# Layer 1's feed-forward input product as seven half products instead of eight

## The chip, the cores and the metric

The kernel runs on one core of one Trainium2 chip. The metric is device time in microseconds (us) of one execution. The engines are named as the profile names them: PE (TensorE, matmuls), DVE (VectorE), ACT (ScalarE), POOL (GpSimd) and SP, whose queue issues the loads of weights.

## The reference, cut to what matters

The model has two layers over 1024 latent tokens (and 256 context tokens, which layer 1 only reads). Layer 1 ends so, with 1024 channels and 2816 hidden columns:

```python
x = _layer_norm(DN_ALPHA * x + g_m * y_lat, ln_g[layer, 0], ln_b[layer, 0])   # y_lat: HGRN2's output projection
f_lat = _conv_ffn(x * (1.0 + sc_f) + sh_f, ffn_w_in[layer], ffn_conv_w[layer],
                  ffn_conv_b[layer], ffn_w_out[layer])
x = _layer_norm(DN_ALPHA * x + g_f * f_lat, ln_g[layer, 1], ln_b[layer, 1])
```

`_conv_ffn` splits u @ w_in (1024 to 2 x 2816) into a and g, runs a centred depthwise convolution of width 3 over the tokens of a, and returns (silu(conv(a)) * g) @ w_out (2816 to 1024). Everything is float32.

## The kernel before, in words

Tokens lie along the free dimension and channels on partitions. A float32 product is made of three matmuls: each operand is held as a high and a low part (`split` L108 to L113: high by ACT L110, low by a subtraction in L113, on POOL for weights and on DVE for `hl`), and `mm3` L100 to L104 adds high times high (L102), high times low (L103) and low times high (L104) in one PSUM bank. The modulated activations u are two tiles, `uh` and `ul`, of [128, 8 channel tiles, 1280 tokens].

Weights come by `wload` (L312 to L325): one transfer of 512 KB by SP into one of two staging places `ws`, then ACT L110 and POOL L113 write the two parts into one of three places `w`.

`ffn` (L1070 to L1180) walks over 22 hidden tiles t of 128 columns. Of each tile, `values` makes the a product for two blocks of 512 tokens (`into`: 8 channel tiles, three matmuls each, into `pa`), and ACT L1118 copies it out; `product` makes the g product the same way into `pg`. `hidden` then runs on DVE and ACT: the convolution in three DVE steps (L1133, L1134, L1135), silu on ACT (L1136), the product with `pg` on DVE (L1137), and the split into `hh` (ACT L110) and `hl` (DVE L113). `out` takes two hidden tiles at a time into `po` (eight pieces of six matmuls for each block), and `gate` (DVE L1065) adds each piece to `acc`.

In front of it stands `Mix1.rest` (the output projection of HGRN2, `pmix`) with `norm` L1013 to L1060 behind each block of columns: sums over channels on PE (`pmean` L1025, `pvar` L1039, `prstd` L591), subtraction, scaling and `rstd` on DVE (L1030, L1045, L578 to L585), the modulated value on ACT, POOL (L1052) and DVE (L1053). The block of tokens 512 to 1024 comes last and in two parts of 256, so the first two hidden tiles run ahead on the tokens that are done. Behind the last hidden tile stand the second `norm` and `store` (L1525 on), which transposes on PE (`pout` L1537) and copies out on ACT (L1538).

The order of the instructions on each engine is not the order of the program text: a scheduler that simulates a timeline sets it, and the pools (places for tiles, banks of PSUM) add the waits.

Of the kernel before, what the change touches and what calls it, by code (L numbers as in the profile page):

```python
# [46 lines left out]
def constants():  # L47
    """Tables that depend on shapes alone."""
# [31 lines left out]
class Pool:  # L80
    """A pool of tiles whose life is not a block of the program text."""
# [12 lines left out]
def raw(t, off, dims):  # L94
    """An access pattern over all partitions of a tile."""
    pstride = t.ap[0][0]
    return bass.AP(tensor=t.tensor, offset=t.offset + off, ap=[[pstride, t.shape[0]]] + dims)


def mm3(nc, ps, w, x, start, stop):  # L100
    """ps (+)= w^T x of float32 operands that come as (hi, lo)."""
# [5 lines left out]
def split(nc, hi, lo, src, ehi="a", elo="p"):  # L107
    """hi = src rounded to twelve bits, lo = the rest: both exact."""  # L108
# [7 lines left out]
def merge(*gens):  # L116
    """Emit the steps of several generators evenly: (number of steps, generator)."""
# [8 lines left out]
def behind(k, inst):  # L126
    """What follows is issued after this instruction, where it is of the same engine."""
# [7 lines left out]
# which banks of PSUM a product goes to: the streams of a phase take theirs apart  # L135
# [9 lines left out]
# ---------------------------------------------------------------- setup  # L145

def setup(k, A):
# [31 lines left out]
    # columns of the small vectors  # L179
# [38 lines left out]
def lower_bounds(k, A, S):  # L218
    """One minus the lower bound of layer 1's forget gates, [128, dir, head]; the masks of its levels."""
# [25 lines left out]
def ada_steps(k, A, pool, layer, c0, nw, wtag=None):  # L245
    """Columns c0 .. c0+4*nw of the modulation of both streams."""
# [60 lines left out]
def wload(k, pool, src, n, tag="w", bufs=3, sbufs=2, elo="p", size=1024, spool=None, stag=None):  # L307
    """A piece of weights [128, kt, m] as (hi, lo)."""
# [13 lines left out]
def exp_small(k, P, o, x, n):  # L322
    """exp to float32's accuracy: 2^k times a polynomial, for a few columns."""
# [22 lines left out]
# ---------------------------------------------------------------- S5 set-up  # L346

def s5_setup(k, A, P, late):
    """late: four places of T columns, in use until this is done."""
# [49 lines left out]
    # powers 0..8 of lambda: [128, part, power, (d p)]  # L399
# [12 lines left out]
    def cmul(o0, n_, a0, b0):  # L412
        """powers o0.. = powers a0.. times power b0"""
# [14 lines left out]
    # input factors (fr, fi)  # L428
# [14 lines left out]
    # the powers for one, two and four chunks of eight tokens  # L443
# [3 lines left out]
    # C, transposed to [(q n), pair, channel]  # L447
# [16 lines left out]
    # B of the discrete system: [(q n), (d pair), channel]  # L464
# [16 lines left out]
    # block diagonal B: [(q n), (q c)] of each pair  # L481
# [11 lines left out]
    for h in range(4):  # L493
        psz[h] = [bank(k, "psz", "C") for d in range(2)]
        for d in range(2):
# [25 lines left out]
            # what a carried state adds to position j: power j+1 forward, 8-j backward  # L521
# [4 lines left out]
            # taps: forward lags 0..7 = index 0..7, backward lags -7..0 = index 1..8  # L526
# [8 lines left out]
            # input matrices: position j enters with power 7-j forward, j backward  # L535
# [26 lines left out]
    # one token of a chunk sees the taps from its own position on  # L562
# [25 lines left out]
def bcast_cols(k, ps, cols, n):  # L588
    """ps[p, 128 i + t] = cols[t, i] for all p."""
# [5 lines left out]
def rot_copy(k, s, kt, m, x0, r0):  # L595
    """staged weights [128, kt, m]: columns r0.. = the rotated partner of columns x0.."""
# [9 lines left out]
def in_proj(k, A, wp, places):  # L606
# [10 lines left out]
    def groups(ms):  # L617
        """The state-space layer's input, eight tokens to a row."""
# [17 lines left out]
    # kr and its rotated partner  # L636
# [54 lines left out]
# ---------------------------------------------------------------- layer 0: attention and S5  # L691

def attention(k, A):
# [18 lines left out]
    # V of all heads  # L712
# [22 lines left out]
    def qk(h):  # L735
# [30 lines left out]
        for s, e in BLK:  # L766
# [14 lines left out]
            # the maximum of every query's scores, negated, in row 96  # L781
# [27 lines left out]
    def attend(h):  # L809
        b = h % 2  # L810
        q, kk_, v = QT[b], KT[b], Vt[b]
        for s, e in BLK:
# [17 lines left out]
            # the sums of the exponentials stay beside the products and divide them later  # L830
# [10 lines left out]
    def inverse(h, s, e):  # L841
        """The reciprocals of two heads' sums."""
# [27 lines left out]
class S5Half:  # L870
    """The state-space layer, sixteen groups at a time, in steps that other work can run between."""
# [802 lines left out]
```

## Time and profile before

| what | value |
|---|---|
| median of three executions | 3871.06 us |
| lowest, highest | 3857.05 us, 3872.54 us |
| the profiled execution: span on the core | 3858.9 us (the page gives no other time of it) |
| PE busy | 3615.2 us, 94% of the span |
| DVE, POOL, ACT busy | 2055.3, 1133.2, 1090.3 us |
| layer 1's feed-forward part, from the end of the last `pmix` to the end | 3044.4 to 3858.9 us |

The span runs from the first to the last instruction that the profiler recorded. The profile names instructions by line, engine and operation, with the tiles that they write and read (out<-in, buffer numbers left out). Matmuls overlap: a matmul of 512 columns is shown as 0.39 us long, while the next one starts 0.23 us later, so the rate is read from starts, or from the count in a window that is 100% busy.

### The profile page before, as it was taken

How to read it: one execution, taken by the hardware profiler on the slowest of the kernel's cores; microseconds unless marked ns; L12 is line 12 of the kernel's file. 1: busy time of each engine (PE TensorE's matmuls, PEld its weight loads, DVE VectorE, ACT ScalarE, POOL GpSimd, SP SyncE). 2: the span in 40 equal slices, each digit the busy share in tenths (PEclk: the TensorE clock that was granted, in tenths of full speed). 3: DMA queues.
4: the chain of work that ended last, by engine and by line, in shares of the span. 5: the costliest groups of instructions: out<-in, count | busy, mean ns of one | idle time of the engine just before them, and what ended most of it. 6: DMA issues, size and time to landing. Idle time of an engine off the chain costs nothing.

```text
span 3858.9 us, 47479 instructions
## 1 busy us (share of the span) xinstructions
PE 3615.2 (94%) x19057; PEld 2924.6 (76%) x19057; DVE 2055.3 (53%) x3297; ACT 1090.3 (28%) x1798; POOL 1133.2 (29%) x1089
## 2 busy tenths in 40 slices
PE   6987999997399999999999899999998999999997
PEld 4764566565278888888888798989887978888886
DVE  7726745773246444444445756464645654444445
ACT  2323435444224111111111522222222421212113
POOL 3617613851144111111112611111112621222222
PEclk8998999998699999999999999999999999999997
DMA  7362335312211111111110201101013111111111
GB/s 239 120 172 80 112 95 134 112 32 94 88 50 44 39 33 39 33 34 49 39 39 28 77 28 33 36 31 39 31 46 95 50 52 42 55 44 50 44 44 44
DMA packets 297079, 245.69 MB, mean 64 GB/s; under 512 B 42488, under 2 KB 257354, under 8 KB 295834
## 3 DMA queue, kind: packets, MB, share of 16 engines
q1 hardware_dynamic: 291930, 229.97, 20.0%
q10 hardware_dynamic: 4928, 12.69, 0.9%
q8 instruction: 149, 2.44, 0.3%
q14 instruction: 72, 0.59, 0.0%
HBM read 206.39 MB, written 38.32 MB: 63 GB/s over the span
## 4 chain that ended last, share of the span: by engine, by line
PE 80%; DVE 6%; DMA 4%; POOL 2%; issue 1%; SPq 1%; ACT 1%; ACTq 0%; DVEq 0%; POOLq 0%
PE pa L104 5%; PE pa L102 5%; PE pa L103 5%; PE po L102 5%; PE pg L102 5%; PE pg L104 5%; PE po L103 5%; PE po L104 5%; PE pg L103 5%; PE ph L103 3%; PE ph L104 3%; PE ph L102 3%; PE pA L1425 3%; PE pY L964 2%; DMA rt<-rsd 2%
## 5 line engine op out<-in xcount | busy, mean ns | idle before, releaser
L113 POOL TENSOR_TENSOR w<-ws,w 128x1024 fp32r<-128x1024 f32 (+1 forms) x205 | 500.2, 2444 | 1570.6 <-ACT w L110 1460.5
L1065 DVE SCALAR_TENSOR_TENSOR acc<-po,mod,acc 128x512 f32<-128x512 f32 (+1 forms) x456 | 309.3, 679 | 560.3 <-PE po L104 560.0
L102 PE MATMUL po<-hh,w 128*128 128x512 f32 (+1 forms) x912 | 342.9, 377 | 9.9 <-DVE acc L1065 8.2
L103 PE MATMUL po<-hl,w 128*128 128x512 f32 (+1 forms) x912 | 336.3, 369 | 5.8 <-DVE hl L113 5.8
L104 PE MATMUL po<-hh,w 128*128 128x512 f32 (+1 forms) x912 | 335.6, 368 | 0.0
L110 ACT ACTIVATE w<-ws 128x1024 fp32r<-128x1024 f32 (+1 forms) x207 | 217.0, 1049 | 409.2 <-PE pg L104 165.7
L102 PE MATMUL pa<-uh,w 128*128 128x512 f32 (+1 forms) x896 | 331.7, 370 | 0.9 <-ACT w L110 0.8
L103 PE MATMUL pa<-ul,w 128*128 128x512 f32 (+1 forms) x896 | 330.1, 369 | 0.1
L104 PE MATMUL pa<-uh,w 128*128 128x512 f32 (+1 forms) x896 | 326.4, 370 | 0.8 <-POOL w L113 0.8
L102 PE MATMUL pg<-uh,w 128*128 128x512 f32 (+1 forms) x872 | 324.1, 372 | 1.9 <-ACT w L110 1.9
L103 PE MATMUL pg<-ul,w 128*128 128x512 f32 (+1 forms) x872 | 322.7, 370 | 0.0
L104 PE MATMUL pg<-uh,w 128*128 128x512 f32 (+1 forms) x872 | 321.5, 372 | 0.6 <-POOL w L113 0.6
L102 PE MATMUL ph<-uh,w 128*128 128x512 f32 (+1 forms) x624 | 239.5, 384 | 1.3 <-ACT uh L1051 1.3
L103 PE MATMUL ph<-ul,w 128*128 128x512 f32 (+1 forms) x624 | 235.6, 378 | 0.8 <-DVE ul L1053 0.8
L104 PE MATMUL ph<-uh,w 128*128 128x512 f32 (+1 forms) x624 | 235.0, 377 | 0.0
L102 PEld LDWEIGHTS po<-hh,w 128*128 128x128 f32 x912 | 174.1, 191 | 45.2 <-DVE acc L1065 11.1
L103 PEld LDWEIGHTS po<-hl,w 128*128 128x128 f32 x912 | 174.4, 191 | 37.9 <-DVE hl L113 6.9
L104 PEld LDWEIGHTS po<-hh,w 128*128 128x128 f32 x912 | 174.2, 191 | 30.3
L102 PEld LDWEIGHTS pa<-uh,w 128*128 128x128 f32 x896 | 168.7, 188 | 32.7 <-ACT w L110 1.0
L104 PEld LDWEIGHTS pa<-uh,w 128*128 128x128 f32 x896 | 168.6, 188 | 32.2 <-POOL w L113 1.3
L103 PEld LDWEIGHTS pa<-ul,w 128*128 128x128 f32 x896 | 168.5, 188 | 32.2 <-DVE ul L1053 0.4
L102 PEld LDWEIGHTS pg<-uh,w 128*128 128x128 f32 x872 | 164.1, 188 | 35.6 <-ACT w L110 2.3
(399 smaller groups left out, 7894.3 us busy)
## 6 DMA issues: line engine op xcount, KB each, us to landing
ws<-in_ffn_w_in_dram SPq DMA_DIRECT2D x88, 512.0 KB
adaw<-in_ada_w_dram SPq DMA_DIRECT2D x80, 512.0 KB
ws<-in_ffn_w_out_dram SPq DMA_DIRECT2D x44, 512.0 KB
ws<-in_hg_w_in_dram SPq DMA_DIRECT2D x40, 512.0 KB
w<-in_ada_w_dram SPq DMA_DIRECT2D x8, 1024.0 KB
ws<-in_ev_w_out_dram SPq DMA_DIRECT2D x10, 512.0 KB
ws<-in_hg_w_out_dram SPq DMA_DIRECT2D x10, 512.0 KB
ws<-in_ev_w_in_dram SPq DMA_DIRECT2D x9, 512.0 KB
```

The source lines that it names most:

```text
L102: nc.tensor.matmul(ps, lhsT=w[0], rhs=x[0], start=start, stop=False)
L103: nc.tensor.matmul(ps, lhsT=w[0], rhs=x[1], start=False, stop=False)
L104: return nc.tensor.matmul(ps, lhsT=w[1], rhs=x[0], start=False, stop=stop)
L110: nc.scalar.activation(hi, src, AF.Copy)
L113: (nc.gpsimd if elo == "p" else nc.vector).tensor_tensor(lo, src, hi.bitcast(F), op=OP.subtract)
L964: nc.tensor.matmul(ps[:, :160], lhsT=O[64 * q:64 * q + 64, d, i], rhs=H[64 * q:64 * q + 64, d:d + 160, d, i, p], start=d == 0 and i == 0, ...
L1065: k.nc.vector.scalar_tensor_tensor(a, ps[:, :e - s], modcol(k, layer, seg, 1 if s >= SEQ else 0, ct), a, op0=OP.mult, op1=OP.add)
L1425: nc.tensor.matmul(ps[:, i * 128:i * 128 + 128], lhsT=km[:, c:c + 128], rhs=raw(Q, c, [[2 * hs, 64 // hs], [SEQ + hs, 2], [1, hs]]), start ...
```

## The change

Layer 1 gets a function of its own, `ffn7`. Two hidden tiles of a (or of g) form a group of 256 columns, so the product of a group is a matrix of 2 x 2 blocks: channel halves against the two hidden tiles (weights A11, A21, A12, A22) and channel halves against the two blocks of tokens (activations B11, B21 and the two of the second block). By Strassen's scheme (in Winograd's form) the four results come from seven half products of 4 x 3 matmuls, 84 in all, where the kernel before ran 96. The operands of the products are A11, A12, A22, S1 = A21 + A22, S2 = S1 - A11, S3 = A11 - A21, S4 = A12 - S2 on the weights' side, and B11, B21, T1, T2, T3, T4 and B22 on the other.

- The S are formed for every group on DVE in the staging places, then split: highs on ACT, lows on DVE for S and on POOL for A11, A12 and A22. A group takes two transfers of 512 KB and four places of the ring `w`, which still has three; the pair's two `w_out` pieces take two more. There are three staging places in place of two.
- The T are formed once, from both blocks, behind the norm: 16 subtractions and 12 lows on DVE, 16 highs on ACT, 4 lows and 4 of B22's on POOL.
- Sums of products are made where possible by accumulating a second product into the same bank; what is left are three to four additions a group on DVE (L1365, L1371, L1393 for a, L1417 for g) and a copy on ACT. The convolution's first step moves from DVE (L1133) to ACT (L1402).
- u is one tile `X` in parts by channel half and block (class `Cols`), so that B's parts are tiles of their own; the norm's temporary tiles share places with `hh` and `hl`. HGRN2's output projection keeps three of its weights instead of four, and loads one a second time. The stretch of memory that is kept for descriptors is set to 1024 bytes.
- `out` has two banks of its own, products turn through the six others. All of the last pair's `out` stands behind the last product.

```diff
+class Seven:
+    def ops(self):
+        k, nc, V, G = self.k, self.k.nc, self.k.nc.vector, self.k.nc.gpsimd
+        for j in range(4):
+            (a, b), t = (r[j] for r in self.raw), self.temps(j)
+            T1, T2, T3, T4 = t
+            V.tensor_tensor(T1, b[:, 0], a[:, 0], op=OP.subtract)
+            V.tensor_tensor(T2, b[:, 1], T1, op=OP.subtract)
+            V.tensor_tensor(T3, b[:, 1], b[:, 0], op=OP.subtract)
+            V.tensor_tensor(T4, a[:, 1], T2, op=OP.subtract)
...
+            for i, (o, x) in enumerate(((self.T2, T2), (self.T3, T3), (self.T1, T1), (self.T4, T4))):
+                split(nc, o[j][:, 0], o[j][:, 1], x, elo="p" if i == 3 else "v")
...
+    def weights(p, i):
...
+        t1, t2, t3 = tile(), tile(), tile()
+        put("A11", t1[0], A11, "p")
+        put("A12", t1[1], A12, "p")
+        put("A22", t3[1], A22, "p")
+        V.tensor_tensor(A22, A21, A22, op=OP.add)
+        V.tensor_tensor(A21, A11, A21, op=OP.subtract)
+        V.tensor_tensor(A11, A22, A11, op=OP.subtract)
+        put("S2", t2[0], A11, "v")
+        put("S3", t2[1], A21, "v")
+        put("S1", t3[0], A22, "v")
+        V.tensor_tensor(A12, A12, A11, op=OP.subtract)
+        t4 = tile()
+        put("S4", t4[0], A12, "v")
...
+        def run(self, begun=False):
...
+            product(b, w["S2"], B.T2, True)
+            V.tensor_tensor(u, u, b, op=OP.add)
+            if not begun:
+                self.second()
+            c = inbank()[:]
+            product(c, w["S3"], B.T3, True)
+            u3 = temp()
+            V.tensor_tensor(u3, u, c, op=OP.add)
+            d = inbank()[:]
+            product(d, w["S1"], B.T1, True)
+            self.to(1, 1, u3, d)
+            product(c, w["A22"], B.T4, False)
+            self.to(1, 0, u, c)
+            product(d, w["S4"], B.B22, False)
+            self.to(0, 1, u, d)
...
+    ga = values(0)
+    ga.first()
+    gg = hidden(0)
+    for p in range(NP):
+        if p == 0:
+            ga.second()
+            ga.run(True)
+        else:
+            ga = values(p)
+            ga.run()
+        if p:
+            ws = [wout(p - 1, i) for i in range(2)]
+            for b in range(2):
+                out(p - 1, ws, b)
+        for j in range(2):
+            conv(p, j)
+        if p:
+            gg = hidden(p)
+        gg.run()
+    ws = [wout(NP - 1, i) for i in range(2)]
+    for b, part in ((0, (0, 512)), (1, (512, 768)), (1, (768, 1024))):
+        out(NP - 1, ws, b, part)
+        done(*part, b == 1)
```

Three places show how the order moves.

PE behind the last `pmix`, around the inverse deviation (`prstd`) of the last 256 tokens. Before, `pa` is the a product of a hidden tile on 256 tokens that are normed already:

```order
L102 MATMUL pa<-uh,w 128x256
L103 MATMUL pa<-ul,w 128x256
L591 MATMUL prstd<-ident,lnr 128x128 x2
L104 MATMUL pa<-uh,w 128x256
L102 MATMUL pa<-uh,w 128x256
```

After, `pi` is any of the seven products, `X_23583` holds T2, the other `X` here T3, and `c_23591` T1:

```order
L1336 MATMUL pi<-X,w 128x512
L1059 MATMUL pvar<-ones,hh 128x1 x4
L611 MATMUL prstd<-ident,lnr 128x128 x2
L1334 MATMUL pi<-X_23583,w 128x512
L1334 MATMUL pi<-X,w 128x512
L1335 MATMUL pi<-X_23583,w 128x512
L1336 MATMUL pi<-X_23583,w 128x512
L1334 MATMUL pi<-X_23583,w 128x512
L1334 MATMUL pi<-c_23591,w 128x512
```

Between the last `pmix` and this `prstd` PE's row had 96 product matmuls of 512 columns and 44 of 256 before; now it has 24 of 512, and the next ones read the T.

DVE in the steady part, between the g product of one pair and what follows. Before, the steps are those of `hidden` and `out`:

```order
L1137 TENSOR_TENSOR c<-c,pg 128x512
L113 TENSOR_TENSOR hl_26431<-c,hh_26430 128x512
L1133 TENSOR_SCALAR c<-a,cols 128x512
L1134 SCALAR_TENSOR_TENSOR c<-a,cols,c 128x512
L1135 SCALAR_TENSOR_TENSOR c<-a,cols,c 128x512
L1133 TENSOR_SCALAR c<-a,cols 128x512
L1065 SCALAR_TENSOR_TENSOR acc<-po,mod_67,acc 128x512
```

After, L1417 and L1418 belong to the g group that ends, L1321 to L1326 are three of the next a group's four sums, the L133 that write `w` are lows of its S, and L1365 and L1371 are additions of its products:

```order
L1417 TENSOR_TENSOR t<-t,pi 128x512
L1321 TENSOR_TENSOR ws<-ws 128x4x128
L133 TENSOR_TENSOR w<-ws,w 128x512
L1418 TENSOR_TENSOR a_23656<-a_23656,t 128x512
L1322 TENSOR_TENSOR ws<-ws 128x4x128
L133 TENSOR_TENSOR w<-ws,w 128x512
L1326 TENSOR_TENSOR ws<-ws 128x4x128
L133 TENSOR_TENSOR hl<-a_23656,hh 128x512
L133 TENSOR_TENSOR w<-ws,w 128x512 x2
L1403 SCALAR_TENSOR_TENSOR c<-a_23950,cols,c 128x512
L1365 TENSOR_TENSOR t<-t,pi 128x512
L1371 TENSOR_TENSOR t<-t,pi 128x512
```

The work on the next group's weights now stands in DVE's row between the last steps of the group before.

PE in the tail, when the first block is normed and goes out. Before, the transposes `pout` come between the pieces of the late parts:

```order
L104 MATMUL po<-hh_28277,w 128x256
L1537 MATMUL pout<-ident,acc 128x128 x4
L102 MATMUL po<-hh_27927,w 128x256
L103 MATMUL po<-hl_27928,w 128x256
L104 MATMUL po<-hh_27927,w 128x256
```

After:

```order
L124 MATMUL po<-hh,w 128x256
L611 MATMUL prstd<-ident,lnr 128x128 x4
L1045 MATMUL pmean<-acc,onesd 128x256
L1809 MATMUL pout<-ident,acc 128x128 x32
L122 MATMUL po<-hh,w 128x256
```

All 32 transposes of the first block stand in one row in front of the remaining pieces of `po`.

## Rows read from the trace of the kernel before

**Rows 1.** The page: the span, and each engine's busy time

```profile
span 3858.9 us, 47479 instructions
PE 3615.2 (94%) x19057; PEld 2924.6 (76%) x19057; DVE 2055.3 (53%) x3297; ACT 1090.3 (28%) x1798; POOL 1133.2 (29%) x1089
```

**Rows 2.** Windows: start:end, length, busy of each engine, clock, DMA share, GB/s

```profile
3080.00:3090.00 10.00, 9.85 (x84) 9.65 (x83) 5.47 (x13) 5.61 (x12) 6.91 (x10) 1.00 0.00 0
3090.00:3100.00 10.00, 8.12 (x35) 5.85 (x34) 9.63 (x9) 4.69 (x8) 5.85 (x4) 1.00 0.32 104
3300.00:3400.00 100.00, 100.00 (x429) 80.44 (x428) 45.86 (x52) 18.84 (x26) 19.84 (x14) 1.00 0.14 43
```

**Rows 3.** Waits, 3150 to 3750: engine, line waited for, total us, times, longest

```profile
POOL w L113 <- ACT w L110: 341.8, 45, 16.7
DVE acc L1065 <- PE po L104: 172.7, 125, 4.6
```

**Rows 4.** Groups by shape, 2700 to 3859: busy us, mean ns | idle before

```profile
L113 POOL TENSOR_TENSOR w<-ws,w 128x1024 fp32r<-128x1024 f32 x82 | 200.4, 2446 | 666.8 <-ACT w L110 556.8 <-PE pa L104 108.6 <-DVE lnv L583 1.3
...
L102 PE MATMUL po<-hh,w 128*128 128x512 f32 x336 | 134.4, 400 | 2.1 <-ACT hh L110 1.5 <-DVE acc L1065 0.4 <-ACT w L110 0.2
...
L1065 DVE SCALAR_TENSOR_TENSOR acc<-po,mod,acc 128x512 f32<-128x512 f32 x168 | 125.7, 749 | 200.4 <-PE po L104 200.4
L110 ACT ACTIVATE w<-ws 128x1024 fp32r<-128x1024 f32 x82 | 86.5, 1056 | 300.0 <-PE pg L104 155.3 <-PE po L104 105.7 <-DMA ws<-in_hg_w_out_dram 28.3
...
L1133 DVE TENSOR_SCALAR c<-a,cols 128x512 f32<-128x512 f32 x44 | 58.7, 1335 | 31.9 <-ACT a L1118 31.5
L1134 DVE SCALAR_TENSOR_TENSOR c<-a,cols,c 128x512 f32<-128x512 f32 x44 | 51.2, 1167 | 2.8 <-DVE c L1133 0.5
...
L113 DVE TENSOR_TENSOR hl<-c,hh 128x512 fp32r<-128x512 f32 x44 | 47.2, 1073 | 16.8 <-ACT hh L110 16.7
...
L1135 DVE SCALAR_TENSOR_TENSOR c<-a,cols,c 128x512 f32<-128x512 f32 x44 | 35.0, 797 | 64.9 <-ACT a L1118 63.7
...
L1137 DVE TENSOR_TENSOR c<-c,pg 128x512 f32<-128x512 f32 x44 | 30.2, 686 | 50.6 <-PE pg L104 49.4 <-ACT c L1136 1.2
...
L110 ACT ACTIVATE hh<-c 128x512 fp32r<-128x512 f32 x44 | 27.7, 629 | 50.5 <-PE po L104 26.7 <-DVE c L1137 23.6
```

**Rows 5.** The chain, 3000 to 3140: start, us, engine, tile, line

```profile
3044.38 1.73 PE pmean L1025 x8
```

**Rows 6.** Timeline of DVE: start, length, line, operation, tiles, count [idle <-releaser]

```profile
3078.34 2.73 DVE L1045 TENSOR_TENSOR acc<-acc,prstd 128x256 f32<-128x256 f32 x8
...
3091.21 3.53 DVE L1134 SCALAR_TENSOR_TENSOR c<-a,cols,c 128x512 f32<-128x512 f32 x2
...
3101.49 2.76 DVE L1134 SCALAR_TENSOR_TENSOR c<-a,cols,c 128x512 f32<-128x512 f32 x1
...
3105.61 0.75 DVE L1134 SCALAR_TENSOR_TENSOR c<-a,cols,c 128x512 f32<-128x512 f32 x1
```

**Rows 7.** Timeline of POOL in the same stretch

```profile
3101.30 2.40 POOL L113 TENSOR_TENSOR w<-ws,w 128x1024 fp32r<-128x1024 f32 x1 [3.55 <-ACT w L110]
```

**Rows 8.** Timeline of PE at the end of the last product

```profile
3789.64 0.40 PE L104 MATMUL pg<-uh,w 128*128 128x512 f32 x1
...
3797.80 0.58 PE L103 MATMUL po<-hl,w 128*128 128x256 f32 x1 [5.80 <-DVE hl L113]
3798.18 0.41 PE L104 MATMUL po<-hh,w 128*128 128x256 f32 x1
3798.39 0.41 PE L103 MATMUL po<-hl,w 128*128 128x256 f32 x1
```

**Rows 9.** The chain, 3740 to the end

```profile
3763.55 0.61 DVE hl L113
...
3769.64 0.73 PE po L102 x2
...
3791.30 4.87 DVE acc L1030 x8
...
3831.95 0.61 ACT os L1538
...
3849.98 3.48 PE pout L1537 x15
```

More of the change, by code (lines that the diff above doesn't have):

```diff
@@ L97, in raw, with __init__, at, latents @@
     return bass.AP(tensor=t.tensor, offset=t.offset + off, ap=[[pstride, t.shape[0]]] + dims)
+class Cols:
+    def __init__(self, pool):
+        self.X = pool([128, 4, 2, 4, 512], R, tag="X")
+        self.pool = pool
+        self.c = [pool([128, 2, 2, 256], R, tag=f"c{i}") for i in range(4)]
+    def at(self, kk, s, e):
+        if s >= SEQ:
+            return [self.c[kk // 2][:, i, kk % 2, s - SEQ:e - SEQ] for i in range(2)]
+        b = s // 512
+        return [self.X[:, 2 * b + kk // 4, i, kk % 4, s - 512 * b:e - 512 * b] for i in range(2)]
+    def latents(self, kk):
+        return [self.X[:, kk // 4:kk // 4 + 3:2, i, kk % 4] for i in range(2)]
 def mm3(nc, ps, w, x, start, stop):
@@ L1187, in ffn, with shared, pool, __init__ @@
     W.free()
+def shared(P):
+    as_ = {"lns": ("hh", 4), "lnq": ("hl", 4)}
+    def pool(shape, dt=F, tag=None, bufs=None):
+        tag, bufs = as_.get(tag, (tag, bufs))
+        return P(shape, dt, tag=tag, bufs=bufs)
+    return pool
+class Seven:
+    def __init__(self, k, u, pool, temps):
+        self.k, self.temps, self.pool, self.cp = k, temps, pool, u.pool
+        X = u.X
+        self.B11, self.B21, self.T3, self.B22 = ([X[:, i, :, j] for j in range(4)] for i in range(4))
+        self.raw = [None, None]
+        self.T1, self.T2, self.T4 = [None] * 4, [None] * 4, [None] * 4
+        self.late = []
+    def rest(self, pool):
+        x = pool([128, 2, 4, 512], R, tag="X6")
+        self.T2 = [x[:, :, j] for j in range(4)]
+        for f in self.late:
+            f()
+        self.ops()
+    def ops(self):
[7 more added lines that the diff above has]
+            V.tensor_tensor(T4, a[:, 1], T2, op=OP.subtract)
+            G.tensor_tensor(self.B22[j][:, 1], b[:, 1], self.B22[j][:, 0].bitcast(F), op=OP.subtract)
+            self.T1[j] = self.cp([128, 2, 512], R, tag=f"c{j}")
+            self.T4[j] = self.pool([128, 2, 512], R, tag=f"X5{j}")
+            for i, (o, x) in enumerate(((self.T2, T2), (self.T3, T3), (self.T1, T1), (self.T4, T4))):
+                split(nc, o[j][:, 0], o[j][:, 1], x, elo="p" if i == 3 else "v")
+    def take(self, x, m0, m1, s, e):
+        k, nc, V, G = self.k, self.k.nc, self.k.nc.vector, self.k.nc.gpsimd
+        n, o, b = e - s, s % 512, s // 512
+        if o == 0:
+            self.raw[b] = [(self.cp, self.pool)[b]([128, 2, 512], tag=f"{('c', 'X5')[b]}{j}") for j in range(4)]
+        for j in range(4):
+            for i in range(2):
+                ct = 4 * i + j
+                r = self.raw[b][j][:, i, o:o + n]
+                G.tensor_scalar(r, x(ct), m0[ct], m1[ct], op0=OP.mult, op1=OP.add)
+                if b and not i:
+                    continue
+                B = (self.B22 if b else (self.B11, self.B21)[i])[j]
+                nc.scalar.activation(B[:, 0, o:o + n], x(ct), AF.Identity, scale=m0[ct], bias=m1[ct])
+                if not b:
+                    V.tensor_tensor(B[:, 1, o:o + n], r, B[:, 0, o:o + n].bitcast(F), op=OP.subtract)
@@ L1502, in states @@
             else:
[L1503 removed]
+                split(nc, *u.at(h, s, e), o[:], elo="v")
         yield 1
@@ L1627, in body, with temps @@
         acc = acc_pool([128, DT, SEQ], tag="acc")
+        B5 = Pool(k, "b5")
+        FP = Pool(k, "ffn1")
+        def temps(j):
+            if j % 2:
+                return [FP([128, 512], tag="hh", bufs=4)[:] for i in range(4)]
+            return [t[:, 512 * i:512 * i + 512] for t in (FP([128, SEQ + 2], tag=f"a{x}", bufs=1) for x in range(2)) for i in range(2)]
+        seven = Seven(k, u, B5, temps)
         W = Pool(k, "wout1")
-        N = Pool(k, "ln1", "right")
         c = coefs(k, 1, 0, (1, 3))
-        mix1.rest(W, acc, lambda s, e, last: norm(k, N, acc, u, c, s, e, last))
+        N = shared(FP)
+        mix1.rest(W, acc, lambda s, e, last: norm(k, N, acc, seven, c, s, e, last))
         W.free()
@@ L1635, in body @@
         c2 = coefs(k, 1, 1, None)
-        O = Pool(k, "out", "right")
+        SX = Pool(k, "ffn1x")
+        seven.rest(SX)
         def fin(s, e, last):
             norm(k, N, acc, None, c2, s, e, last)
-            store(k, O, acc, out, s, e, last)
-        ffn(k, A, u, acc, 1, SEQ, fin, O)
+            store(k, lambda shape, tag, bufs: SX(shape, tag="X6", bufs=1), acc, out, s, e, last)
+        ffn7(k, A, seven, acc, 1, fin, FP, SX)
         mark("ffn1")
-        O.free()
-        N.free()
+        SX.free()
+        FP.free()
+        B5.free()
         acc_pool.free()
         k.WP.free()
-        u_pool2.free()
         u_pool.free()
```

149 lines of the change are left out of this document (127 added, 22 removed).

## The prediction, written before the changed kernel had run

> **What bounds the kernel now.** I read the page first: PE is busy for 3615.2 us of a span of 3858.9 [rows 1]. The windows say what that means in the stage that changes. In 3300 to 3400 PE is busy for all 100.00 us and runs 429 matmuls of 512 columns, so one costs 100 / 429 = 0.2333 us, while DVE is busy for 45.86 us, ACT for 18.84 and POOL for 19.84 [rows 2]. Third come the waits: POOL waits for ACT, DVE for PE [rows 3], and no wait of PE is in that view. So a matmul that goes away there is worth its 0.2333 us, and a wait put before PE costs its full length. Last I read the two ends of the stage: its start is the end of the last `pmix`, T0 = 3044.4 [rows 5], its last product starts at 3789.64 and so ends, at the rate, near 3790 [rows 8].
>
> From T0 to that product are 745 us. By the code they hold 22 x 2 x 48 = 2112 product matmuls (492.7 us) and 3 x 336 = 1008 of `po` ([rows 4], 235.2 us), 727.9 in all; 17 us are other things: sums of the norms, and a hole of some 6 us before 3769.64, where PE waits for the last tiles' convolution [rows 9]. Behind that product comes a tail of 69 us.
>
> **The change part by part.**
>
> *Products.* 22 groups of 84 are 1848 matmuls, 264 fewer: 264 x 0.2333 = -61.6 us. `X` is read in runs of 512 columns and the weights in runs of 128, as before, so the rate stays. On the path, all of it.
>
> *The start.* Before, PE had 96 + 44/2 = 118 matmuls' worth (27.5 us) to run while the last 256 tokens were normed, and the window in which they are split is 9.85 busy of 10 [rows 2]. Now it has 24. The T need all tokens, normed. DVE's last scaling ended at 3078.34 + 2.73, T0 + 36.7 [rows 6], with steps of the first hidden tiles and of PE's long row between; DVE's own steps (two blocks, two passes of 2.73, some 6 us of deviations, and a wait for PE's sums) cannot come under 20. I take T0 + 27. Then stand 28 steps of 512 columns on DVE (16 subtractions, 12 lows), at 0.686 (L1137) to 1.073 (`hl`) [rows 4], 19 to 30 us; I take 24, between the two since POOL works beside them. PE can run some 60 matmuls (14 us) by then. So 27 + 24 - 14 = 37 us of the start are no product; the ends are 20 + 19 - 14 = 25 and 36.7 + 30 - 14 = 53.
>
> *The steady pairs.* A pair is now 168 + 96 = 264 matmuls, 61.6 us (before, 288 and 67.2). On DVE it has 34 steps of two tensors (8 sums and 8 lows of the S, 4 of `hl`, 4 of L1365 and L1371, 10 more of the results), 8 of the convolution and 16 gates: 11 read PSUM, at 0.686; 23 read SBUF alone, at 0.68 to 1.07; the convolution costs 0.75 to 1.17 each and the gates 0.749 [rows 4, 6]. That is 41 to 53 us of 61.6, where 4 x (1.335 + 1.167 + 0.797 + 0.686 + 1.073) + 16 x 0.749 = 32 of 67.2 were. ACT gains small highs and stays near a third; POOL has 6 lows of half a size and 2 whole ones, 6 x 1.22 + 2 x 2.446 = 12 us. None is over PE's 61.6. What costs is the ring of three places: a pair takes ten, before six, and some are taken so that their last reader and first user stand next to each other in PE's row. I count three such places a pair: the next a group's A11 and S1 (its places were S2, S3 and S1 of the g group; ACT 0.629, then a low of 0.686 to 1.073), the first `w_out` piece (it takes S2's and S3's place; ACT 1.056 for 1024 columns, and the hand-over), and the lows of A11 by POOL (half of 2.446) with u3, which must be read before A22's product goes into its bank (0.686) [rows 4]. At about 1.6 us each that is 4.8 us a pair. With another product in PE's row before each only about 2 are left; with a POOL low in front of each DVE step (2.446 more for the three, and their queue) about 9. I take 4.8 x 10 = 48 us, ends 20 and 90.
>
> *POOL beside DVE.* The same DVE step takes 0.75 us alone and 2.76 when a POOL low of 2.40 runs beside it [rows 6, 7]: it ends when POOL does. The Trainium skill ("GPSIMD Engine Reference", section 1, Specifications) states that GpSimd's SBUF interface is shared with VectorE and contends with DVE steps that have two SBUF inputs; the trace agrees, with these 2.0 us. The 16 sums and lows of the S in a pair are such steps, and eight POOL lows a pair can meet them. This speaks against the change, and it is the second rival's mechanism.
>
> *The tail.* Before, all of the first block's last `po` ran before the last product (its norm begins at 3791.30 [rows 9]), and the 67.6 us from there to the end are the norm, the transposes and the two late parts. Now 48 matmuls (11.2 us) and the sums (some 2 us) come behind the product, and the same chain may follow: 13 + 67.6 = 81 us. All 32 transposes then stand in one row before the remaining `po`, on one bank, with a copy of 0.61 on ACT for every four [rows 9]: about 8 x 1.3 = 10 us that parts of the late pieces used to fill. I take 87, ends 80 and 92.
>
> *At nothing:* the fourth `w_out1` piece, loaded twice (under the `pmix` products; 1.06 + 2.45 us [rows 4] and the transfer if they are not cover), the same bytes of weights through three staging places (the DMA share is 0.14 [rows 2]), and the size of the descriptors' memory.
>
> *Sum from T0.* Products 431.2, `po` before the last product 960 x 0.2333 = 224.0, start 37, steady 48: 740, against 745. Tail 87 against 69. So -5 + 18 = **+13 us**. The 61.6 us are nearly all given back. The profiled span of 3858.9 would become 3872; it lies among the three executions (3857.05 to 3872.54), so I add the difference to the median: 3871.06 + 13 = **3884 us**. About 0.5%, 19 us, is what a measurement of this kernel can tell from no change.
>
> **The rivals.**
>
> *A, faster: the ring is no wait.* If the scheduler's row leaves another product in front of PE at most hand-overs, a pair waits for 2 us (20 in all); with a start of 33 and a tail of 82 the sum is 431.2 + 224.0 + 33 + 20 - 745 + 82 - 69 = -24, **3847 us**. For it: nothing but PE is over 86% of a pair. Against: the before never has four sums and their lows between two products.
>
> *B, slower: DVE behind POOL sets the pair.* S2 needs S1, a subtraction and a low in turn, and the lows share DVE's row with gates, additions and the convolution. If a step of it meets a POOL low each time (2.0 us [rows 6]), 2 more a group go on the path, 4 a pair: 8.8 x 10 is 40 over my sum, +53, **3924 us**. It decides once a pair's waits pass 5.5 us (20 us over no change at 10 pairs). For it: DVE at up to 53 of 61.6 and stretches like 9.63 of 10 busy with PE at 8.12 [rows 2]. Against: half of POOL's lows are half as long now.
>
> *C: the products are not what the time is made of.* If the seven products ran no faster than the eight (reads of the split tiles costing more), only the additions would stay: +13 + 61.6, 3946 us. Nothing in the rows speaks for it.
>
> *D: the clock.* Behind a wait of 5.80 us PE starts matmuls of 256 columns 0.21 us apart [rows 8], nearly double half of 0.2333: the granted clock is at the lower of its two levels there. In 3090 to 3100, with 1.9 us idle, it stays at 1.00 [rows 2]. So the steady waits cost no clock; the holes at the start may cost about 2 to 4 us, which lie in its ends.
>
> **How the numbers follow.** Forecast (-19 to +19 us) 0.42; A and what is faster still 0.22; B with its lesser forms 0.34; C 0.02. The predicted time is 3884. The range leaves out about one in ten on each side: from A, 3846, to B, 3926. Faster by over 0.5% is A, 0.22; the same 0.42; slower is B and C, 0.36. The forecast's own range is 3852 to 3890.
>
> **What the profile of the changed kernel would show.** PE's matmul count falls by 264. Right behind T0, a stretch of some 50 us in which PE is busy for under half, waiting for DVE's lows of the T. In the steady pairs PE is busy for 92 to 94%, a pair lasts 66 us, DVE is busy for 41 to 53 us of it, and PE's waits name ACT, DVE or POOL writing `w`. In the tail one row of 32 `pout`, and 80 to 92 us behind the last product. I am wrong if pairs last under 64 us (then A), over 68 (then B, with DVE steps of 2 us and more beside POOL's lows), or if the start's loss is outside 25 to 53 us.

## The result, and the profile after

The changed kernel takes 3893.63 us (median of four, 3889.11 to 3897.43) against 3870.84 us before, so it is 22.8 us slower by the medians. The ratio estimated from all executions is 1.0072, 95% interval 1.0052 to 1.0091. The profiled execution has a span of 3891.2 us, 32.3 more than [rows 1].

Three windows hold layer 1's feed-forward part of the changed kernel: the start, from the end of the last `pmix` (T0) until PE runs without a hole; the pairs; and the tail from the last product. Columns as in [rows 2].

```profile
3051.20:3106.05 54.85, 29.55 (x91) 20.86 (x89) 49.13 (x88) 25.81 (x49) 39.77 (x43) 0.66 0.06 20
3106.05:3782.36 676.31, 654.84 (x2756) 514.80 (x2755) 424.54 (x610) 213.83 (x331) 147.88 (x125) 1.00 0.15 48
3782.36:3891.20 108.84, 70.71 (x293) 55.62 (x291) 51.08 (x120) 28.09 (x53) 19.64 (x24) 0.68 0.10 39
```

The same of the kernel before, up to its last product and behind it:

```profile
3044.40:3789.88 745.48, 741.59 (x3262) 599.05 (x3262) 365.64 (x459) 159.68 (x232) 183.87 (x142) 1.00 0.14 44
3789.88:3858.90 69.02, 44.56 (x243) 39.46 (x241) 40.91 (x108) 28.15 (x53) 16.24 (x21) 0.74 0.15 61
```

So T0 to the end of the products went from 745.5 to 731.1 us, which is 14.4 less, and the tail from 69.0 to 108.8, which is 39.8 more. The remaining 6.8 us lie in front of T0. They are no larger than what this stretch differs by from run to run: the last `pmix` matmul starts at 3044.1 and 3051.3 in the two traces of the kernel before and of its one variant below, and anywhere from 3041.2 to 3053.7 in the eleven traces of the changed kernel and its variants. Without these 6.8 the difference is 25.4, near that of the medians. From here on a kernel is read by two numbers: from the start of the last `pmix` matmul to the start of the last product matmul (before 745.5, after 731.1), and from there to the end, the tail (before 69.3, after 109.1). The ends of the first number, before and after; that of the last product before is in [rows 8]:

```profile
3044.10 0.28 PE L104 MATMUL pmix<-uh,w 128*128 128x256 f32 x1
...
3050.97 0.28 PE L124 MATMUL pmix<-X,w 128*128 128x256 f32 x1
...
3782.12 0.40 PE L1336 MATMUL pi<-X,w 128*128 128x512 f32 x1
```

**The start.** DVE's timeline: the norm's last scaling, the first of the 28 steps that form the T, two beside POOL, and the last.

```profile
3073.87 2.73 DVE L1065 TENSOR_TENSOR acc<-acc,prstd 128x256 f32<-128x256 f32 x8 [1.38 <-PE prstd L611]
3076.53 0.68 DVE L1250 TENSOR_TENSOR a<-X,c 128x512 f32<-128x512 f32 x1
...
3091.12 1.76 DVE L1251 TENSOR_TENSOR hh<-X,hh 128x512 f32<-128x512 f32 x1
3092.81 1.75 DVE L1252 TENSOR_TENSOR hh<-X 128x512 f32<-128x512 f32 x1
...
3104.20 0.68 DVE L133 TENSOR_TENSOR c<-hh,c 128x512 fp32r<-128x512 f32 x1
```

PE in the same stretch: the last product that needs no T, the wait for the T, and two neighbours.

```profile
3062.18 0.39 PE L1336 MATMUL pi<-X,w 128*128 128x512 f32 x1
...
3080.51 1.40 PE L1334 MATMUL pi<-X,w 128*128 128x512 f32 x2 [6.68 <-ACT X L130]
...
3088.36 0.63 PE L1335 MATMUL pi<-X,w 128*128 128x512 f32 x1
3088.78 0.63 PE L1336 MATMUL pi<-X,w 128*128 128x512 f32 x1
```

The scaling ends 25.4 us behind T0, the steps take until 3104.88, and the matmuls in between start 0.42 us apart: they run at the lower level of the clock.

**The pairs.** PE's waits from 3106 to 3782 (engine, line waited for, total, times, longest):

```profile
PE po L122 <- ACT w L130: 12.6, 11, 1.1
PE pi L1334 <- ACT w L130: 7.2, 10, 0.7
PE pi L1336 <- DVE w L133: 1.7, 10, 0.2
```

Three waits a pair, all for a weight that is just being written into the ring: for a `w_out` piece, for A11's high part, and for S1's low part. By the rate, the 2754 product matmuls of this window are 642.5 of the 676.3 us; 33.8 are these waits (21.5 in sum) with what they cost at their edges.

**The tail.** DVE's two passes of each norm (L1050 subtracts, L1065 scales) in the changed kernel:

```profile
3800.07 4.87 DVE L1050 TENSOR_TENSOR acc<-acc,pmean 128x512 f32<-128x512 f32 x8 [3.19 <-PE pmean L1045]
3818.70 4.87 DVE L1065 TENSOR_TENSOR acc<-acc,prstd 128x512 f32<-128x512 f32 x8 [1.22 <-PE prstd L611]
3848.83 2.73 DVE L1050 TENSOR_TENSOR acc<-acc,pmean 128x256 f32<-128x256 f32 x8 [0.81 <-PE pmean L1045]
...
3871.09 2.73 DVE L1050 TENSOR_TENSOR acc<-acc,pmean 128x256 f32<-128x256 f32 x8 [0.81 <-PE pmean L1045]
```

Before, the first block's passes stood at 3791.30 [rows 9] and 3810.34, and the late parts' followed at once:

```profile
3810.34 4.87 DVE L1045 TENSOR_TENSOR acc<-acc,prstd 128x512 f32<-128x512 f32 x8 [0.84 <-PE prstd L591]
...
3815.53 2.73 DVE L1030 TENSOR_TENSOR acc<-acc,pmean 128x256 f32<-128x256 f32 x8
...
3829.64 2.74 DVE L1030 TENSOR_TENSOR acc<-acc,pmean 128x256 f32<-128x256 f32 x8 [1.25 <-PE pmean L1025]
```

Cut in three: from the last product to the first pass 1.7 us before and 18.0 after, which is the first block's `out` (+16.3); from there to the end of the scaling 23.9 and 23.5; from there to the end 43.7 and 67.6 (+23.9). PE shows what fills the last piece:

```profile
3805.09 0.55 PE L122 MATMUL po<-hh,w 128*128 128x256 f32 x1 [5.05 <-DVE acc L1050]
...
3823.71 1.09 PE L1809 MATMUL pout<-ident,acc 128*128 128x128 f32 x4 [4.30 <-DVE acc L1065]
3825.58 1.09 PE L1809 MATMUL pout<-ident,acc 128*128 128x128 f32 x4 [0.78 <-ACT X L1810]
...
3838.38 0.58 PE L122 MATMUL po<-hh,w 128*128 128x256 f32 x1 [0.74 <-ACT X L1810]
...
3851.62 0.38 PE L122 MATMUL po<-hh,w 128*128 128x256 f32 x1 [2.83 <-DVE acc L1050]
```

Pieces of `out` wait for L1050, which reads the bank of `pmean`. They do not use its result: `out` has banks 6 and 7 here, and these are the banks of `pmean` (6) and of `pvar`, `prstd` and the transposes (7). Before, it had 4 and 5 to itself.

### The profile page after: what moved, and what is told of

Its sections match the earlier page's. It is cut to its first block, busy times and chain, and to the rows that moved or that the text cites. A ratio compares the mean times of both kernels' runs of the same rounds, so it can differ in the third digit from the quotient of the medians.

```text
span 3891.2 us, 47196 instructions
## 1 busy us (share of the span) xinstructions
PE 3590.3 (92%) x18697; PEld 2876.7 (74%) x18697; DVE 2179.1 (56%) x3551; ACT 1170.9 (30%) x1948; POOL 1145.9 (29%) x1120
## 4 chain that ended last, share of the span: by engine, by line
PE 76%; DVE 8%; DMA 4%; POOL 3%; issue 2%; ACT 2%; SPq 1%; ACTq 0%; DVEq 0%; POOLq 0%
PE po L122 5%; PE po L124 5%; PE po L123 5%; PE pi L1336 3%; PE pi L1334 3%; PE ph L123 3%; PE pi L1335 3%; PE ph L124 3%; PE ph L122 3%; PE pA L1697 3%; PE pa L122 3%; PE pa L124 3%; PE pa L123 3%; PE pg L122 3%; PE pg L124 3%; PE pg L123 3%
## 5 line engine op out<-in xcount | busy, mean ns | idle before, releaser
L133 POOL TENSOR_TENSOR w<-ws,w 128x1024 fp32r<-128x1024 f32 (+2 forms) x229 | 494.9, 2170 | 1557.0 <-ACT w L130 1554.6
L130 ACT ACTIVATE w<-ws 128x1024 fp32r<-128x1024 f32 (+2 forms) x319 | 266.7, 845 | 541.9 <-PE po L124 176.6
L122 PE MATMUL po<-hh,w 128*128 128x512 f32 (+1 forms) x912 | 343.2, 377 | 35.0 <-DVE acc L1088 13.5
L1334 PE MATMUL pi<-X,w 128*128 128x512 f32 x528 | 213.1, 404 | 20.7 <-ACT X L130 12.2
L1335 PE MATMUL pi<-X,w 128*128 128x512 f32 x528 | 211.5, 401 | 1.8 <-DVE X L133 1.8
L1336 PE MATMUL pi<-X,w 128*128 128x512 f32 x528 | 204.6, 401 | 0.0
L122 PE MATMUL ph<-X,w 128*128 128x512 f32 x496 | 202.8, 409 | 1.3 <-ACT X L1074 1.3
L123 PE MATMUL ph<-X,w 128*128 128x512 f32 x496 | 199.2, 402 | 0.8 <-DVE X L1076 0.8
L124 PE MATMUL ph<-X,w 128*128 128x512 f32 x496 | 199.5, 402 | 0.0
L133 POOL TENSOR_TENSOR pl<-p,ph 128x512 fp32r<-128x512 f32 (+1 forms) x88 | 116.9, 1329 | 233.8 <-ACT ph L130 103.4
L815 DVE TENSOR_REDUCE mx<-pS 128x1 f32<-128x512 f32 (+1 forms) x168 | 110.5, 684 | 71.6 <-PE pS L812 71.2
L122 PE MATMUL pg<-X,w 128*128 128x512 f32 x352 | 140.1, 398 | 1.9 <-ACT w L130 1.9
L122 PE MATMUL pa<-X,w 128*128 128x512 f32 x352 | 140.1, 398 | 0.0
L123 PE MATMUL pa<-X,w 128*128 128x512 f32 x352 | 139.6, 396 | 0.0
L123 PE MATMUL pg<-X,w 128*128 128x512 f32 x352 | 139.4, 396 | 0.0
L124 PE MATMUL pg<-X,w 128*128 128x512 f32 x352 | 138.4, 398 | 0.6 <-POOL w L133 0.6
```

The costliest lines, as they stand in the source:

```text
L122: nc.tensor.matmul(ps, lhsT=w[0], rhs=x[0], start=start, stop=False)
L123: nc.tensor.matmul(ps, lhsT=w[0], rhs=x[1], start=False, stop=False)
L124: return nc.tensor.matmul(ps, lhsT=w[1], rhs=x[0], start=False, stop=stop)
L130: nc.scalar.activation(hi, src, AF.Copy)
L133: (nc.gpsimd if elo == "p" else nc.vector).tensor_tensor(lo, src, hi.bitcast(F), op=OP.subtract)
L815: nc.vector.tensor_reduce(mx[:, t:t + m, j:j + 1], ps[:].rearrange("p (m x) -> p m x", m=m), axis=AX.X, op=OP.max, negate=True)
```

## The experiments

Theory: the changed kernel loses in the tail because `out`, the norm and the transposes share two banks; the start is DVE's 28 steps, and the pairs' waits are the ring of three places. Rivals stand in the expectations. Tails and times to the last product are those defined above, each from one profiled execution. They repeat: in the seven traces whose products are those of the changed kernel the time to the last product is 731.1 to 731.5 us, and the tail is 108.0 to 111.1 in the four traces that leave it as it is.

**The tail: one part of the banks at a time.** `po_abc`:

```diff
-            ps = bank(k, "po", "DE")
+            ps = bank(k, "po", "ABC" if p == NP - 1 else "DE")
```

> One edit to the changed kernel: the pieces of `out` of the last pair go to the six product banks (0 to 5) instead of the two banks 6 and 7 that the norm's sums (`pmean`, `pvar`, `prstd`) and the transposes use. In the changed kernel 108.8 us lie between the last product's start (3782.4) and the end, against 69.0 before. Theory of the banks: the late pieces stand behind the norm's readers (5.05 and 2.83 us of PE's waits there name L1050), and the 32 transposes stand in front of them because of that; with banks of their own the tail falls by 17 to 24 us, to 85 to 92, and the kernel's time by as much, to some 3873. Rival, the late start: the tail is long because all of the first block's `out` begins only after the last product and because PE runs at the lower clock; then the banks change it by under 5 us and it stays at 104 to 109.

`pout_ab`:

```diff
-            ps = bank(k, "pout", "AB" if last else "E")
+            ps = bank(k, "pout", "AB")
```

> One edit to the changed kernel: the transposes of the first two parts take turns in banks 0 to 3, where only those of the last part did; `out` keeps banks 6 and 7. In the changed kernel the 32 transposes of the first block take 14.7 us in one row (3823.71 to 3838.38), each four waiting 0.7 us for ACT's copy out of the one bank. Theory of the banks: the row goes at PE's pace, 8 x 1.1 = 9 us, and no longer stands as one piece, so the tail falls by 6 to 10 us, less than by the other edit, since the pieces of `out` still share two banks with the norm. Rival, the late start: under 3 us.

`both_banks` makes both edits.

> Both edits of the banks at once: `out` of the last pair in banks 0 to 5, all transposes in banks 0 to 3. Theory of the banks: at least the better of the two alone, a tail of 82 to 90 us and a time of 3866 to 3876; what is left over 69 is the first block's `out` behind the last product (48 matmuls, 11 us). Rival, the late start: 100 to 109 us.

Measured: tails of 96.7, 93.5 and 99.8 us (109.1 without them), 731.5, 731.2 and 731.4 us to the last product, ratios to the kernel before of 1.0048 (1.0033 to 1.0063), 1.0037 (1.0024 to 1.0051) and 1.0053 (1.0038 to 1.0068). So the edits take 12.4, 15.6 and 9.3 us off the tail. The first two are more than the rival allows (under 5 and under 3), but none lies in the theory's range: the first gives less than expected, the second more, and both together are worse than either and end beside the rival's 100 to 109. The theory as it stood was too simple. The order of the runs shows why the two edits do not add up. With `out` in six banks the scheduler puts pieces of both late parts in front of the first block's norm and leaves the 32 transposes in one row; with both edits the row of 32 stands too. In `both_banks` PE first waits long for the first norm's sums, and then pieces of `out` wait behind the row of transposes:

```profile
3802.42 3.70 PE L1059 MATMUL pvar<-ones,hh 128*128 128x1 f32 x16 [9.06 <-POOL hh L1056]
...
3812.13 6.27 PE L1809 MATMUL pout<-ident,acc 128*128 128x128 f32 x24 [1.65 <-POOL acc L1082]
3818.88 1.14 PE L1809 MATMUL pout<-ident,acc 128*128 128x128 f32 x8 [0.48 <-ACT X L1810]
3824.49 0.58 PE L122 MATMUL po<-hh,w 128*128 128x256 f32 x1 [4.47 <-ACT X L1810]
```

**The tail: the sharing itself taken away.** `norm_banks` leaves `out` its two banks and moves everything else out of them:

```diff
-    pm = bank(k, "pmean", "D")
+    pm = bank(k, "pmean", on[0])
...
-            norm(k, N, acc, None, c2, s, e, last)
+            norm(k, N, acc, None, c2, s, e, last, "ABB")
...
-            ps = bank(k, "pout", "AB" if last else "E")
+            ps = bank(k, "pout", "C")
```

(`on` is "DEE" for all other norms; `pvar` and `prstd` take its second and third letter.)

> Banks of the tail parted otherwise: the last norm's `pmean` in banks 0 and 1, its `pvar` and `prstd` in 2 and 3, the transposes in 4 and 5, and `out` alone in 6 and 7. In the changed kernel the tail (from the last product's start to the end) is 109.1 us, and the second part's norm begins 22.3 us behind the first's, 48.8 us behind the first block's. Theory of the banks: what is left of the extra 40 us beside the late first block (16 us) comes from pieces that wait for a bank; with four separate pairs PE's row has no long run of transposes, the second part's norm begins under 15 us behind the first's, and the tail falls to 78 to 88 us, the time by 21 to 31. Rival (the row of 32 transposes alone): as in the run that only gave the transposes four banks, 93 us.

Measured: a tail of 69.8 us, 731.3 to the last product, and a ratio of 0.9971 (0.9961 to 0.9982) to the kernel before: 39.3 us of tail gone, more than expected, and the change is now a small gain of 0.3%. `norm_banks_aff` and `s4_place` below, with the same banks, have tails of 72.6 and 71.8. The reason given came only in part: rows of up to 20 transposes still stand together, and the second part's norm begins 16.4 us behind the first's, not under 15. DVE's passes in its tail, the late parts' between the first block's two and right behind them:

```profile
3806.10 4.87 DVE L1050 TENSOR_TENSOR acc<-acc,pmean 128x512 f32<-128x512 f32 x8 [0.81 <-PE pmean L1045]
3816.03 2.74 DVE L1050 TENSOR_TENSOR acc<-acc,pmean 128x256 f32<-128x256 f32 x8 [0.37 <-PE pmean L1045]
3827.36 4.87 DVE L1065 TENSOR_TENSOR acc<-acc,prstd 128x512 f32<-128x512 f32 x8 [0.18 <-PE prstd L611]
3832.43 2.72 DVE L1050 TENSOR_TENSOR acc<-acc,pmean 128x256 f32<-128x256 f32 x8
```

The first block's pass comes even later than in the changed kernel (21.1 us behind the last product, against 18.0). What the sharing had cost was the overlap of the three norms with each other and with the late pieces, not the late first block: from the first pass to the end it is 48.7 us here, 91.1 in the changed kernel, 67.6 before. The clock went with it. The whole tail as a window, to be read beside that of the changed kernel above:

```profile
3785.00:3854.80 69.80, 55.84 (x294) 44.42 (x292) 49.70 (x120) 26.62 (x53) 19.86 (x24) 0.89 0.15 61
```

The granted clock is 0.89 in place of 0.68, and PE is busy for 55.84 us with as many matmuls as in 70.71 there. So of the 39 us some 15 are matmuls that run at the higher level for more of the tail, and some 24 are time in which PE stands still (38 us there, 14 here). No run changes the one without the other, and none moves the norm's sums alone: `pout_ab` had 15.6 us from the transposes' banks, and the other 23.7 came with the sums' banks and the order that goes with them.

**Is a transposes' bank worth the same before?** `before_ab` makes `pout_ab`'s edit in the kernel before.

> The kernel before with one edit: all transposes in banks 0 to 3, as in the run that gave them to the changed kernel (15.6 us of its tail). Before, the tail from the last product is 69 us and PE waits for a copy out of the one bank some four times, 0.25 to 0.84 us each. Theory: before, the pieces of `out` have banks of their own (4 and 5) and stand between the transposes, so the one bank costs under 3 us, and the kernel stays at its time within 0.1%. Rival, that the transposes' bank is worth the same in any order: 8 to 15 us less.

Measured: a ratio of 1.0030 (1.0018 to 1.0042), 11 us slower; neither was expected. PE's timeline shows the reason: the scheduler now puts the first block's norm and all 32 transposes in front of the last 24 matmuls of the last product, so PE waits there for the norm's sums and for the copies out, with little left to run beside them.

```profile
3801.97 3.69 PE L1039 MATMUL pvar<-ones,lns 128*128 128x1 f32 x16 [9.06 <-POOL lns L1036]
...
3818.43 1.15 PE L1537 MATMUL pout<-ident,acc 128*128 128x128 f32 x8 [0.47 <-ACT os L1538]
3821.82 0.80 PE L102 MATMUL pg<-uh,w 128*128 128x512 f32 x1 [2.24 <-ACT os L1538]
```

The same edit takes 15.6 us off the tail of one kernel and adds 11 us to the time of the other: the worth of a bank is that of the order which it makes.

**The start.** `no_t` leaves out the forming of T1 to T4; their products read B22.

```diff
-            (a, b), t = (r[j] for r in self.raw), self.temps(j)
-            T1, T2, T3, T4 = t
-            V.tensor_tensor(T1, b[:, 0], a[:, 0], op=OP.subtract)
...
+            a, b = (r[j] for r in self.raw)
             G.tensor_tensor(self.B22[j][:, 1], b[:, 1], self.B22[j][:, 0].bitcast(F), op=OP.subtract)
...
+        self.T1 = self.T2 = self.T3 = self.T4 = self.B22
```

> Leaves out the forming of T1 to T4 (16 subtractions and 12 lows on DVE, 16 highs on ACT, 4 lows on POOL); the four products that read a T read B22 in its place, so they still wait for the normed last block and do as many matmuls. In the changed kernel the start lasts 54.9 us (3051.2 to 3106.05) with 60 matmuls, 14 us, in it, and DVE's 28 steps end at 3104.9. Theory: these steps stand on the path, so 20 to 28 us go from the start and from the time, to some 3868. Rival: the norm's chain and the lower clock set the start, and only 5 to 10 us go.

Measured: 715.5 us to the last product, 15.6 less: between the two expectations. The steps are on the path, but of the 28 us that they take PE gets back little more than half; PE's last long wait there is for B22's low on POOL (3.27 us), behind the norm.

`aff_only` issues the norm's closing affine steps behind the forming of the T:

```diff
+    if isinstance(u, Seven):
+        u.later.append(affine)
+    else:
+        affine()
```

> One edit to the changed kernel: the affine steps that finish the norm in front of layer 1's feed-forward part (8 steps on POOL and 8 on ACT for the last block, and those of the first) are issued behind the forming of the T, so that POOL makes the T's last lows and B22's earlier, and fewer POOL steps run beside DVE's 28. In the changed kernel T0 (end of the last `pmix`) to the last product's start is 731.1 us. Theory of POOL beside DVE: six of the 28 DVE steps take 1.75 us beside POOL steps in place of 0.68, so 3 to 7 us go, 724 to 728. Rival, the count of DVE steps alone: under 2 us.

Measured: 731.3 us, no gain. This run does not decide, because the scheduler kept POOL's four affine steps of the last block about where they had been (3076.3 to 3094.1, 24 to 42 us behind T0; without the edit 24 to 40), and DVE steps still took 1.76 us beside POOL. The edit also aimed at the wrong steps: in both traces all DVE steps of 1.5 us and more stand beside POOL's subtractions for B22 and T4 (L1254 and L133 in the changed kernel), and beside the affine steps DVE takes 0.68 to 1.0. `norm_banks_aff` joins it with the parted banks.

> Both: the parted banks of the tail and the late affine steps. If the two are independent, the sum of both: a tail of 78 to 88 us and 724 to 728 us from T0 to the last product, so 24 to 38 us less than the changed kernel, which is 5 to 12 us under the kernel before. If the tail's gain depends on the rest of the order, less than 20 us.

Measured: 731.2 us to the last product and a tail of 72.6, ratio 0.9976 (0.9966 to 0.9986): the banks' gain alone.

**The pairs.** `no_s` leaves out the S; their products read A11 and A22, and a group takes two places of the ring.

```diff
-        put("S2", t2[0], A11, "v")
-        put("S3", t2[1], A21, "v")
-        put("S1", t3[0], A22, "v")
...
+        ops["S2"] = ops["S3"] = ops["A11"]
+        ops["S1"] = ops["S4"] = ops["A22"]
```

> Leaves out the sums S1 to S4 on the weights' side with their highs and lows, and with them two of the four places of the ring `w` that a group takes: their products read A11 and A22 in place of the S, as many matmuls as before. In the changed kernel 3106.05 to 3782.36 is 676.3 us for 2748 matmuls of 0.2333 us (641.1), so 35 us of waits; 27 of them name ACT's highs of `w` and 10 DVE's lows, 1 us each. Theory of the ring: nearly all of the 35 us go, T0 to the last product falls by 28 to 35. Rival, DVE's load: if additions and gates set the waits, under 15 go.

Measured: 692.4 us to the last product, 38.7 less: the whole of the waits in the pairs and some of the start. (By the list above those waits are 31 and not 37: 21 name ACT's highs, and the ten that name DVE's lows are 0.2 us each.) It took DVE's load away too, so the next run keeps that. `s4_place`, on top of `norm_banks`, gives S4 a place of its own in exchange for the third staging place:

```diff
-        t4 = tile()
-        put("S4", t4[0], A12, "v")
+        put("S4", SX([128, 2, 512], R, tag="s4", bufs=1), A12, "v")
```

> On top of the parted banks of the tail: S4 gets a place of its own (4 KB, in exchange for the third staging place), so a group takes three places of the ring `w` and a pair eight in place of ten. With the parted banks T0 to the last product's start is 731.3 us and the tail 69.8. Leaving out the S took 38.7 us from the first of these, but with them went DVE's load as well as the ring's places. Theory of the ring: `w_out` can take A11's and A12's place early, its 11 waits of 1.1 us and more go, and one more product runs ahead at the start (2.8 us): 12 to 20 us less, 711 to 719. Rival, DVE's load or the transfers: with DVE's work unchanged and a staging place less, under 4 us less, or more than before.

Measured: 714.7 us to the last product, 16.6 less with the same steps on DVE, and 3835.07 us against 3865.53 of the kernel before on that chip: a ratio of 0.9925 (0.9911 to 0.9938). It beats both kernels. The two ends of its first number (S4's product reads tile `s`), and PE's waits in its pairs:

```profile
3049.91 0.28 PE L124 MATMUL pmix<-X,w 128*128 128x256 f32 x1
...
3764.60 0.39 PE L1335 MATMUL pi<-X,s 128*128 128x512 f32 x1
```

```profile
PE po L122 <- ACT w L130: 6.4, 10, 0.7
PE pi L1333 <- DVE t L1370: 2.3, 9, 0.3
PE pi L1335 <- POOL w L133: 0.4, 1, 0.4
```

The `w_out` wait is halved, and those for A11 and for S1's low no longer appear; what is new is a wait of 0.3 a pair for L1370, the addition that frees a bank. In sum PE's waits in the pairs are 9.1 us in place of 21.5. The product more that runs ahead at the start brought nothing: the last low of the T ends 57.4 us behind T0 here and 53.8 in `norm_banks`. So most of the pairs' waits came from the ring and not from DVE's load.

`s4_ahead` also issues A11·B11 and A12·B21 of the first g group ahead of the T.

> The same, and the second of the two products of the first g group that need no T is also issued ahead of the T, so that 48 matmuls in place of 24 stand between the last `pmix` and the first product with a T. Theory of the start: PE is idle there behind DVE, so each matmul that moves ahead is worth its 0.2333 us: 12 of them 2.8 us more than the run beside it, 24 of them 5.6 us. Rival: the norm's sums wait behind them on PE and the T come as much later; no gain.

Measured: 716.6 us to the last product, no gain; ratio 0.9937 (0.9923 to 0.9950). The rival was nearer, in another form: with the g group's weights earlier, its four sums (L1320 to L1326) stand in DVE's row between the steps of the T, and the last low of the T ends 59.5 us behind T0, 2.1 later than in `s4_place`.

## Why the prediction was right or wrong, point by point

The time lies in the range (3846 to 3926), 10 us above the forecast, but the likeliest case was "no change a measurement can tell", and the kernel is slower by 0.72%: the case that came had the smaller chance, 0.36, and its mechanism was not the one I gave it. That the time came so near is in part luck: the pairs were put 14 us too high, the start 4 and the tail 22 too low, and these errors cancel for the greater part.

- *Products, -61.6: right.* The sum from T0 to the last product was 740 and is 731; the rate of 0.2333 us held.
- *The start, 37 us: right in mechanism, 41 measured.* 54.9 us with 58 product matmuls (13.5) in them. The scaling ended at T0 + 25.4 (27 taken) and the 28 steps took 28.3 us (24 taken), since eight of them ran at 1.56 to 1.76 us beside POOL's subtractions.
- *The pairs, 48 us: right in mechanism, too large.* 33.8 us, 3.4 a pair in place of 4.8. Of the three places of the forecast two are in PE's own waits: the first `w_out` piece (1.15 us), and the next group's A11 and S1, which show as two waits (0.72 and 0.17). The third, POOL's lows of A11 with u3, shows no wait. DVE is busy for 424.54 of 676.3 us, 63%, or 40.6 of a pair of 64.7, just under the 41 to 53 that I worked out, because its steps run nearer to their time alone (L133 into `w` at 0.686). PE is busy for 97% there, not 92 to 94.
- *The tail, 87 us, ends 80 and 92: wrong, 109.* This is the term that failed. "The same chain may follow" added 67.6 us behind the first block's `out`; I allowed 6 us for the row of 32 transposes and looked at one bank only. The diff says that `out` takes "DE", and the norm's lines say "D" and "E" for the sums; I costed the transposes' share of bank 7 and not that every late piece of `out` waits for the norm's readers, and the norms for each other. Against the kernel before, 23.9 us stand there where 6 were allowed, and 16.3 us of late first block where 11 were. `norm_banks` shows it by taking the sharing away, which gives back 39.3 us.
- *In front of T0, nothing: not contradicted.* The 6.8 us there are within the 12.5 by which that stretch differs among the eleven traces of the changed kernel and its variants.
- *The signs.* A pair of 64.7 us is between 64 and 68, and a start's loss of 41 between 25 and 53, so no sign of being wrong showed: I had set none for the tail. PE's count fell by 360 and not by 264, since the 96 matmuls more that the first two hidden tiles ran in parts of 256 went too.
- *Rival A* had the pairs with hardly a wait: not in this kernel. `s4_place` with the tail parted comes near to it in the pairs (9.1 us of waits, some 17 with their edges, for A's 20) and passes its time by the tail.
- *Rival B* (DVE behind POOL sets the pair): wrong. The mechanism is in the rows of the start, and in the pairs the convolution's second step L1404 has a mean of 0.997 us where alone it takes 0.74; but PE's waits name it nowhere. The step in [rows 6, 7] also did not end when POOL's did, as I read it, but 0.55 us later (3104.25 and 3103.70). The Trainium skill's sentence on the shared interface (GPSIMD Engine Reference, section 1, Specifications) agrees with the 1.75 us that DVE's steps with two operands in SBUF take in the start, and it did not decide the time.
- *Rival C*: wrong, by the rate.
- *Rival D*: the lower clock was there, 0.66 of full speed over the start and 0.68 over the tail. At the start it costs about 2 us, an estimate from the ten matmuls around DVE's last lows, which start 0.43 us apart in place of 0.23. In the tail it goes with about 15 of the 39 us that the sharing costs; that PE's standing still there brings it is likely, but no run shows it by itself. I had put it at the start alone, and at 2 to 4 us.

## What to carry to other kernels

When a stage loses its cover, look at who shares its buffers before adding up its work: the change put `out` into the two banks of the norm and the transposes, and that cost 39 us of a tail in which nothing else was left to run. A ring that feeds more and smaller operands needs places, not engine time: one more place of half size was worth 16.6 us where DVE had 37% to spare. Where a scheduler sets the order, an edit's worth is that of the order that it makes; try it in the kernel at hand, since the same line gave 16 us of tail here and cost 11 there.

## What the runs showed of the hardware

POOL and DVE slow each other, and which of them loses more depends on POOL's step. A POOL `tensor_scalar` of 256 columns (L1270) takes 0.55 us at 3063.15, while DVE's steps (L1065) read one of their two operands from PSUM, and 2.02 at 3082.74, while DVE works through steps with both operands in SBUF. Those DVE steps lose little by it: 0.68 to 1.06 us, where they take 0.68 with POOL all but idle (L133 at 3104.20, above). Beside POOL's subtraction of two operands (L1254) the same DVE steps take 1.75 us, and the subtraction takes 1.7 where it takes 1.26 with DVE idle (L133 at 3095.79 in `aff_only`). Of POOL and, between them, of DVE in the changed kernel:

```profile
3063.15 1.10 POOL L1270 TENSOR_SCALAR X<-acc,lnm 128x256 f32<-128x256 f32 x2
...
3081.21 0.68 DVE L1252 TENSOR_TENSOR hh<-X 128x512 f32<-128x512 f32 x1
...
3082.74 2.02 POOL L1270 TENSOR_SCALAR X<-acc,lnm 128x256 f32<-128x256 f32 x1
...
3090.64 3.37 POOL L1254 TENSOR_TENSOR X<-X,X 128x512 fp32r<-128x512 f32 x2
```

and of POOL in `aff_only`:

```profile
3095.79 1.26 POOL L133 TENSOR_TENSOR X<-a,X 128x512 fp32r<-128x512 f32 x1
```
